# One more up-projection group as seven products, and six operand pairs of the down-projection split by ScalarE and an accumulating DMA inside SBUF

## The chip, the cores and the metric

The kernel runs on one core of one Trainium2 chip. The metric is device time in microseconds (us), the median over several executions; a profile of one further execution goes with it. The engines are named as the profile names them: PE is TensorE (matmuls; PEld is the load of its stationary operand), DVE is VectorE, ACT is ScalarE, POOL is GpSimd, SP is SyncE, which only starts DMAs here.

## The reference

The reference is an encoder trunk of two layers over 512 tokens with a model width of 1024. Each layer has a block of four parallel branches (a convolution and three attentions), which the change does not touch, and then this feed-forward part:

```python
D_MODEL = 1024
SEQ = 512
DEPTH = 2
D_FF = 2816
...
ConvFFN: RMSNorm -> up-projection -> depthwise conv width 3 -> SwiGLU -> down-projection, residual add
```

The up-projection maps the 1024 normalised channels to 2 x 2816, a gate half and an up half. Each of these channels goes through a convolution of width 3 along the tokens. The gate half goes through Silu and is multiplied with the up half, which gives 2816 channels f; the down-projection maps f back to 1024, and the residual is added. All is float32.

## The kernel before

**How a matmul is written.** Operands are split into a high part (a copy that rounds to the fast matmul format) and a low part (the value minus the high part), and each product is made of three matmuls: high by high, high by low, low by high (`prod`, L290 to L292). For every weight unit ACT writes the high part (`w_hi`, L269 or L1277) and DVE the low part (`w_lo`, L271 or L1278), from a staging tile that a DMA has filled. There are three buffers of each, and a unit is asked for two units ahead of its use (`unit`, L275). So PE waits for DVE when a low part comes late.

**The up-projection.** The 2 x 2816 output channels are 22 column tiles of the gate half (s = 0) and 22 of the up half (s = 1). Two neighbouring tiles of both halves are a group; there are 11 groups. A "whole" step (`block`, L308) makes one tile of one half with 24 matmuls of 512 columns; then DVE moves it out of PSUM (L1216, `U<-mm`) and `conv_part` (L1163) runs the convolution: one ACT operation and two of DVE (L1171 to L1173), then Silu on ACT for the gate half (L1177, `fth`), or the product f on DVE for the up half (L1185). A group in `SEVEN` is made by Strassen's scheme instead: seven products of half the size in place of eight, each a step of 24 matmuls of 256 columns (`seven`, L1113, matmul L1130). The sums of its inputs are made once per layer (`seven_forms`, L1071). The sums of its weights are made one after the other in the staging tile, by a DMA from POOL's queue that adds a quarter of the weights to what is there (`grow`, L1258, an accumulating DMA of 512 KB, named `chain<-W` or `w_raw<-W`); high and low parts are split off each time (L1277, L1278). So a group takes 7 x 24 matmuls of 256 columns where the whole form takes 4 x 24 of 512 columns. `UP_STEPS` is the order of all these steps: whole groups 0 and 1, the seven-product groups 2 to 7 interleaved, then the rest whole; the first two blocks after the seven-product groups are made early and held in PSUM.

**The down-projection.** It too runs in Strassen's form, over pairs j = 0 to 10 of two f tiles. The loop over j (`down`, L1369) uses per pair two weight units of 12 matmuls of 512 columns each (L1376 to L1378). Before that, `split_pair` (L1330) makes a pair's operands: three 256-column sums on DVE (L1357 to L1359, and L1363), four copies on ACT for the high parts (L1354) and four subtractions on DVE for the low parts (L1355); two of the four of each are the 512-column halves of the pair itself (`ih`, `kh` high; `il`, `kl` low). For six pairs, those that `EARLY` names by the tile at which they are made, this runs inside the up-projection; for the others it runs in the loop over j, one pair per turn. `pair_tags` (L1313) says in which buffers the operands go: the low parts of a later pair j lie in the buffer `fp{j-1}`, which held the f of pair j - 1.

**What sets the order.** Instructions are put in order per engine by a list scheduler that goes by its own estimates. `first()` (L304) gives those inside it priority. In the second, last layer `turn_res` (L1224) also moves the residual through DVE transposes and 32 DMAs of 64 KB (`resT<-xn`) during the up-projection.

Of the kernel before, what the change touches and what calls it, by code (L numbers as in the profile page):

```python
# [3 lines left out]

# [2 lines left out]

# [5 lines left out]
F32 = mybir.dt.float32  # L15
F32R = mybir.dt.float32r
I32 = mybir.dt.int32
AF = mybir.ActivationFunctionType
ALU = mybir.AluOpType
# [3 lines left out]
P = 128  # L23
L = 2
D = 1024
S = 512
# [3 lines left out]
NF = DFF // P  # L30
# [2 lines left out]

CHUNK = 4

SEVEN = (2, 3, 4, 5, 6, 7)


def up_steps():

    whole = lambda g: [('whole', 2 * g + i, s) for i in range(2) for s in range(2)]
    slots = {}
    for i, g in enumerate(SEVEN):
        for n, at in (('A11', 0), ('S3', 4), ('A22', 6), ('S2', 8), ('A12', 9), ('S1', 10), ('S4', 12)):
            slots[7 * i + at] = ('seven', g, n)
    steps = [w for g in range(SEVEN[0]) for w in whole(g)]
    after = [w for g in range(SEVEN[-1] + 1, NP2) for w in whole(g)]
    own = [slots[t] for t in sorted(slots)]
# [8 lines left out]
              ('gb', 'A22'), ('ga', 'S2'), ('ga', 'S1'), ('gb', 'S2'), ('gb', 'S1'), ('ga', 'S4'), ('gb', 'S4')]  # L57
MIX = (0, 1, 4, 5, 2, 3, 6, 7)

EARLY = (15, 16, 17, 18, 19, 20)  # L60
EPS = 1e-6
BIG = 1e30
EB = 4
# [35 lines left out]
def weight_units():  # L99
# [19 lines left out]
    for g in range(NP2):  # L119
        if g in SEVEN:  # L120
            units.extend(('quarter', (g, r, c), 1024) for r in range(2) for c in range(2))
# [109 lines left out]
class Trunk:  # L231
# [931 lines left out]
    def conv_part(self, i, s):  # L1163

        nc = self.nc
        v = nc.vector
        c = i + s * NF
        u = self.U[s][:, i % 2]
        y = self.fp.tile([P, S], F32, name=f"cy{s}", tag=f"cy{s}", bufs=2)
        w = lambda t: self.par('ffn_conv_w', c * 3 + t)  # L1170
        nc.scalar.activation(y, u[:, 1:513], AF.Identity, scale=w(1), bias=self.par('ffn_conv_b', c))  # L1171
        v.scalar_tensor_tensor(y, u[:, 0:512], w(0), y, ALU.mult, ALU.add)
        v.scalar_tensor_tensor(y, u[:, 2:514], w(2), y, ALU.mult, ALU.add)  # L1173

        if s == 0:
            si = self.fp.tile([P, S], F32, name="fth", tag="fth", bufs=2)
            nc.scalar.activation(si, y, AF.Silu)  # L1177
            self.silus[i] = si
            return
        if self.last and i % 2 == 1 and i // 2 < KT:  # L1180
            self.turn_res(i // 2)
        if i % 2 == 0:
            self.fpair = self.fp.tile([P, 1024], F32, name="f", tag=f"fp{i // 2}", bufs=1)
        fl = self.fpair[:, i % 2 * S:(i % 2 + 1) * S]
        v.tensor_tensor(fl, y, self.silus.pop(i), ALU.mult)  # L1185
        self.F.append(fl)
        if i in EARLY:
            self.split_pair(self.F, EARLY.index(i), self.got)

    def ffn(self, l, last):  # L1190
        nc = self.nc
        v = nc.vector
        self.U = []
        for i in range(2):
            u = self.conv_tile(f"U{i}")
            nc.gpsimd.memset(u[:, :, 0:1], 0.0)
            nc.gpsimd.memset(u[:, :, 513:514], 0.0)
            self.U.append(u)
        self.F, self.got, self.silus, self.sevens, self.last = [], {}, {}, {}, last
        self.seven_forms()  # L1200
        held = {}
        self.pace = 0.0
        for kind, a, b in UP_STEPS:
            if kind == 'seven':
                self.seven(a, b)
                continue
            if kind == 'free':
                ps = held.pop((a, b))
            else:
                ps = self.mm()  # L1210
                self.block(ps)
                self.tick()
            if kind == 'held':
                held[a, b] = ps
            else:
                v.tensor_tensor(self.U[b][:, a % 2, 1:513], ps, self.RB, ALU.mult)  # L1216
                self.conv_part(a, b)
        for g in self.slow:
            for _ in g:
                pass  # L1220
        self.slow = []
        return self.F
# [90 lines left out]
    def pair_tags(self, j):  # L1313

        x = [f"x{n}{d}" for d in range(KT) for n in 'hl']
        late = [(f"lt{n // 2}", n % 2) for n in range(10)]
        hi = [f"fh{2 * j}", f"fh{2 * j + 1}"] if j < len(EARLY) else x[2 * (j - len(EARLY)):][:2]
        lo = ["lo", "lo"] if j == 0 else [(f"fp{j - 1}", 0), (f"fp{j - 1}", 1)]  # L1320
        a = (["e0", "e1"], ["e2", "e3"], ["e4", "e5"], late[0:2], late[2:4], late[4:6],
             ["xr", "xr"], ["xn", "xn"], ["cy0", "cy0"], ["cy1", "cy1"], x[10:12])[j]
        s4 = (late[6:8], late[8:10], ["e6", "e7"], x[12:14], x[14:16], ["t3", "t2"])[j // 2]
        return hi + lo + a + s4

    def conv_tile(self, tag):
# [3 lines left out]
    def split_pair(self, F, j, got):  # L1330

        nc = self.nc
        v = nc.vector
        fi, fk = F[2 * j:2 * j + 2]

        def tile(t):
            if isinstance(t, tuple):
                t, n = t
                if n == 0:
                    self.halves[t] = self.fp.tile([P, 1024], F32R, name=f"p{t}", tag=t, bufs=1)  # L1340
                return self.halves[t][:, n * S:(n + 1) * S]
            pool = self.xpool if t[:2] in ("xh", "xl") else self.fp
            return pool.tile([P, S], F32R, name=f"p{t}", tag=t, bufs=2 if t in ("lo", "xr", "xn", "cy0", "cy1") else 1)

        tags = self.pair_tags(j)
        ih, kh, il, kl, ah, al = (tile(t) for t in tags[:6])
        if j % 2 == 0:
            got['b'] = [tile(t) for t in tags[6:]]
        lo, hi = slice(0, 256), slice(256, 512)
        bh, bl = (t[:, (lo, hi)[j % 2]] for t in got['b'])  # L1350
        a = self.fp.tile([P, S], F32, name="sum", tag="xr" if j < len(EARLY) else "fth", bufs=2)

        def split(h, l, x):
            nc.scalar.activation(h, x, AF.Copy)  # L1354
            v.tensor_tensor(l, x, h.bitcast(F32), ALU.subtract)  # L1355

        v.tensor_tensor(a[:, lo], fi[:, hi], fk[:, hi], ALU.subtract)  # L1357
        v.tensor_tensor(fi[:, hi], fi[:, lo], fi[:, hi], ALU.subtract)
        v.tensor_tensor(a[:, hi], a[:, lo], fi[:, lo], ALU.subtract)  # L1359
        split(ih, il, fi)  # L1360
        split(ah, al, a)
        split(kh, kl, fk)
        v.tensor_tensor(fk[:, lo], fk[:, lo], a[:, hi], ALU.add)  # L1363
        split(bh, bl, fk[:, lo])
        cut = lambda h, l, c: [(h[:, c + b * P:c + (b + 1) * P], l[:, c + b * P:c + (b + 1) * P]) for b in range(2)]
        got[j] = {'a11': cut(ih, il, 0), 's1': cut(ih, il, 256), 'a12': cut(kh, kl, 0), 's4': cut(kh, kl, 256),
                  's3': cut(ah, al, 0), 's2': cut(ah, al, 256), 'a22': cut(bh, bl, 0)}

    def down(self, F, last):  # L1369
# [9 lines left out]

        got, todo = self.got, list(range(len(EARLY), NP2))  # L1380
        A, B = ([self.mm() for _ in range(2)] for _ in range(2))
# [315 lines left out]
```

## Time and profile before

| | us |
|---|---|
| median of three runs | 1542.93 (1542.21 to 1543.67) |
| the profiled execution | 1543.59 |
| its span, first to last instruction | 1541.8 |
| outside the span | 1.79 |
| up-projection of layer 0, from 433.42 to 663.98 | 230.56 |
| up-projection of layer 1, from 1200.20 to 1433.09 | 232.89 |

Times inside the program are counted from the first instruction. T0 below is the end of an up-projection's last matmul and the start of the loop over j. In the windows of the profile a column gives an engine's busy time and in brackets its instructions, then TensorE's granted clock, the busy share of the 16 DMA engines, and what they moved.

### The profile page before, as it was taken

How to read it: one execution, taken by the hardware profiler on the slowest of the kernel's cores; microseconds unless marked ns; L12 is line 12 of the kernel's file. 1: busy time of each engine (PE TensorE's matmuls, PEld its weight loads, DVE VectorE, ACT ScalarE, POOL GpSimd, SP SyncE). 2: the span in 40 equal slices, each digit the busy share in tenths (PEclk: the TensorE clock that was granted, in tenths of full speed). 3: DMA queues.
4: the chain of work that ended last, by engine and by line, in shares of the span. 5: the costliest groups of instructions: out<-in, count | busy, mean ns of one | idle time of the engine just before them, and what ended most of it. 6: DMA issues, size and time to landing. Idle time of an engine off the chain costs nothing.

```text
span 1541.8 us, 22905 instructions
## 1 busy us (share of the span) xinstructions
PE 1528.9 (99%) x8274; PEld 1322.0 (86%) x8274; DVE 1308.0 (85%) x2210; ACT 942.8 (61%) x1580; POOL 187.7 (12%) x288
## 2 busy tenths in 40 slices
PE   9999999999999999999999999999999999999999
PEld 8888888889889999888888888888898899988887
DVE  6689988797789999996576899887986899999974
ACT  6677777356456665564548687673564566655643
POOL 0123002321001110000002130023200011100000
PEclk9999999999999999999999999999999999999999
DMA  7789586856656886366568795867566589852674
GB/s 236 227 229 203 164 181 152 181 151 148 208 168 141 178 182 162 96 205 203 180 185 255 203 202 174 171 161 182 146 150 215 171 173 230 182 155 96 191 229 161
DMA packets 117153, 278.58 MB, mean 181 GB/s; under 512 B 27440, under 2 KB 29360, under 8 KB 117040
## 3 DMA queue, kind: packets, MB, share of 16 engines
q1 hardware_dynamic: 87088, 187.98, 38.2%
q0 software_dynamic: 29664, 88.62, 30.5%
q8 instruction: 65, 1.06, 0.3%
q10 hardware_dynamic: 288, 0.52, 0.1%
q14 instruction: 48, 0.39, 0.1%
HBM read 259.25 MB, written 58.72 MB: 206 GB/s over the span
## 4 chain that ended last, share of the span: by engine, by line
PE 85%; DVE 8%; ACT 3%; issue 2%; DMA 2%; POOL 0%; ACTq 0%; DVEq 0%; POOLq 0%
PE mm L291 14%; PE mm L290 14%; PE mm L292 14%; PE aux L1130 11%; PE aux L936 3%; PE aux L1376 3%; PE aux L1378 3%; PE aux L1377 3%; PE mm L520 2%; PE mm L521 2%; PE mm L522 2%; PE mm L1376 2%; PE mm L1378 2%; PE mm L1377 2%; PE mm L1130 2%
## 5 line engine op out<-in xcount | busy, mean ns | idle before, releaser
L269 ACT ACTIVATE w_hi<-w_raw 128x1024 fp32r<-128x1024 f32 (+1 forms) x241 | 251.1, 1043 | 232.5 <-PE mm L291 83.3
L271 DVE TENSOR_TENSOR w_lo<-w_raw,w_hi 128x1024 fp32r<-128x1024 f32 (+1 forms) x241 | 290.5, 1207 | 72.8 <-ACT w_hi L269 71.3
L290 PE MATMUL mm<-xh,w_hi 128*128 128x512 f32 x768 | 300.2, 391 | 0.0
L291 PE MATMUL mm<-xl,w_hi 128*128 128x512 f32 x768 | 299.5, 390 | 0.0
L292 PE MATMUL mm<-xh,w_lo 128*128 128x512 f32 x768 | 299.3, 390 | 0.0
L292 PEld LDWEIGHTS mm<-xh,w_lo 128*128 128x128 f32 x768 | 144.2, 188 | 30.6
L290 PEld LDWEIGHTS mm<-xh,w_hi 128*128 128x128 f32 x768 | 144.3, 188 | 29.0
L291 PEld LDWEIGHTS mm<-xl,w_hi 128*128 128x128 f32 x768 | 144.3, 188 | 28.3
L1130 PE MATMUL aux<-form,w_hi 128*128 128x256 f32 x768 | 140.2, 283 | 1.4 <-ACT sv L1142 1.4
L1130 PEld LDWEIGHTS aux<-form,w_hi 128*128 128x128 f32 x768 | 120.0, 192 | 2.5 <-ACT sv L1142 2.2
L1130 PE MATMUL aux<-form,w_lo 128*128 128x256 f32 x384 | 108.7, 283 | 0.0
L1277 ACT ACTIVATE w_hi<-chain 128x1024 fp32r<-128x1024 f32 x64 | 67.6, 1057 | 53.7 <-DMA chain<-W 11.5
L457 DVE SCALAR_TENSOR_TENSOR cv<-cv,prm 128x512 f32<-128x512 f32 x120 | 94.6, 788 | 0.7
L1278 DVE TENSOR_TENSOR w_lo<-chain,w_hi 128x1024 fp32r<-128x1024 f32 x64 | 77.9, 1219 | 17.0 <-ACT w_hi L1277 16.7
L1171 ACT ACTIVATE cy<-U,prm 128x512 f32<-128x512 f32 x88 | 68.4, 808 | 32.2 <-DVE U L1216 21.0
L520 PE MATMUL mm<-w_hi,xh 128*128 128x512 f32 x192 | 76.4, 398 | 0.3 <-DVE V L648 0.3
L1277 ACT ACTIVATE w_hi<-w_raw 128x1024 fp32r<-128x1024 f32 x48 | 50.6, 1053 | 42.4 <-PE aux L1130 21.1
L521 PE MATMUL mm<-w_lo,xh 128*128 128x512 f32 x192 | 74.9, 390 | 0.0
L522 PE MATMUL mm<-w_hi,xl 128*128 128x512 f32 x192 | 74.8, 390 | 0.0
L1259 POOL DMA_DIRECT2D chain<-W x48 | 42.1, 876 | 260.4 <-DVE w_lo L1278 233.1
L1130 PEld LDWEIGHTS aux<-form,w_lo 128*128 128x128 f32 x384 | 73.7, 192 | 0.0
L777 ACT ACTIVATE e<-e,rl 128x256 f32<-128x256 f32 (+2 forms) x96 | 57.3, 597 | 21.8 <-DVE rl L776 21.5
(376 smaller groups left out, 3837.7 us busy)
## 6 DMA issues: line engine op xcount, KB each, us to landing
w_raw<-W SPq DMA_DIRECT2D x191, 512.0 KB, 4.1
sums<-W POOLq DMA_DIRECT2D x24, 1024.0 KB, 11.5
chain<-W POOLq DMA_DIRECT2D x48, 512.0 KB, 5.7
w_raw<-W SPq DMA_DIRECT2D x66, 256.0 KB, 3.7
w_raw<-sums SPq DMA_DIRECT2D x44, 256.0 KB, 3.8
w_raw<-sums SPq DMA_DIRECT2D x22, 512.0 KB, 4.3
sums<-W POOLq DMA_DIRECT2D x12, 768.0 KB, 10.7
sums<-sums POOLq DMA_DIRECT2D x8, 1024.0 KB, 7.2
```

The source lines that it names most:

```text
L269: w = nc.scalar.activation(hi[:, s], raw[:, s], AF.Copy)
L271: nc.vector.tensor_tensor(lo[:, s], raw[:, s], hi[:, s].bitcast(F32), ALU.subtract)
L290: mm(ps, lhsT=wh, rhs=xh, start=start, stop=False)
L291: mm(ps, lhsT=wh, rhs=xl, start=False, stop=False)
L292: self.last_mm = mm(ps, lhsT=wl, rhs=xh, start=False, stop=stop)
L457: self.after_mm(v.scalar_tensor_tensor(acc, u[:, t:t + S], w(t), acc, ALU.mult, ALU.add))
L520: mm(pss[b], lhsT=self.Xh[k][:, t], rhs=hi[:, s], start=k == 0, stop=False)
L521: mm(pss[b], lhsT=self.Xh[k][:, t], rhs=lo[:, s], start=False, stop=False)
L522: self.last_mm = mm(pss[b], lhsT=self.Xl[k][:, t], rhs=hi[:, s], start=False, stop=k == KT - 1)
L1130: self.last_mm = nc.tensor.matmul(o, lhsT=w[:, s], rhs=x, start=start and not (e or j or i), stop=j == 3 and i == 2, skip_group_check=True)
L1277: nc.scalar.activation(hi, raw, AF.Copy)
L1278: nc.vector.tensor_tensor(lo, raw, hi.bitcast(F32), ALU.subtract)
```

## The change

1. `SEVEN` takes in group 8 (tiles 16 and 17): in each layer four whole steps go and seven seven-product steps come.
2. `EARLY` becomes a list of steps (tile, half), and the six pairs that are made during the up-projection go through the new `early_pair`. Sums and the operands `ah`, `al`, `bh`, `bl` are made as before. The pair itself is one tile of 1024 columns now: ACT copies it to `hi` and then writes minus `hi` to `low`, and an accumulating DMA of POOL's queue, 512 KB from SBUF to SBUF, adds the pair to `low`. This stands in place of two 512-column copies on ACT and two 512-column subtractions on DVE. The low part of pair j lies in `fp{j-2}` (for pairs 0 and 1 in buffers of their own), and the two halves of the 256-column operand of pair 10 lie in `fp4`.
3. The move out of PSUM of the last four blocks (tiles 20 and 21) stands under `first()`.

```diff
-SEVEN = (2, 3, 4, 5, 6, 7)
+SEVEN = (2, 3, 4, 5, 6, 7, 8)
...
-EARLY = (15, 16, 17, 18, 19, 20)
+EARLY = ((17, 1), (19, 0), (19, 1), (20, 0), (20, 1), (21, 0))
...
-        if i in EARLY:
-            self.split_pair(self.F, EARLY.index(i), self.got)
+        if (i, 1) in EARLY:
+            self.early_pair(EARLY.index((i, 1)))
+
+    def early_pair(self, j):
...
+        f = self.fpairs[j]
+        tags = self.pair_tags(j)
+        hi = self.fp.tile([P, 1024], F32R, name="pfh", tag=f"fh{j}", bufs=1)
+        low = self.fp.tile([P, 1024], F32R, name="plo", tag=f"fp{j - 2}" if j > 1 else f"lo{j}", bufs=1)
...
+        v.tensor_tensor(a[:, :256], q(1), q(3), ALU.subtract)
+        v.tensor_tensor(q(1), q(0), q(1), ALU.subtract)
+        nc.scalar.activation(hi, f, AF.Copy)
+        nc.scalar.activation(low, hi.bitcast(F32), AF.Copy, scale=-1.0)
+        nc.gpsimd.dma_start(low, f, accum_op=ALU.add)
+        v.tensor_tensor(a[:, 256:], a[:, :256], q(0), ALU.subtract)
+        b = self.fp.tile([P, S], F32, name="sum", tag="xr", bufs=2)[:, :256]
+        v.tensor_tensor(b, q(2), a[:, 256:], ALU.add)
+        nc.scalar.activation(ah, a, AF.Copy)
+        v.tensor_tensor(al, a, ah.bitcast(F32), ALU.subtract)
+        nc.scalar.activation(bh, b, AF.Copy)
+        v.tensor_tensor(bl, b, bh.bitcast(F32), ALU.subtract)
...
-                v.tensor_tensor(self.U[b][:, a % 2, 1:513], ps, self.RB, ALU.mult)
+                with self.first() if a >= NF - 2 else nullcontext():
+                    v.tensor_tensor(self.U[b][:, a % 2, 1:513], ps, self.RB, ALU.mult)
...
-        lo = ["lo", "lo"] if j == 0 else [(f"fp{j - 1}", 0), (f"fp{j - 1}", 1)]
+        lo = [(f"fp{j - 1}", 0), (f"fp{j - 1}", 1)]
...
-        s4 = (late[6:8], late[8:10], ["e6", "e7"], x[12:14], x[14:16], ["t3", "t2"])[j // 2]
+        s4 = (late[6:8], late[8:10], ["e6", "e7"], x[12:14], x[14:16], [("fp4", 0), ("fp4", 1)])[j // 2]
```

In the changed kernel the lines of `early_pair` are L1207, L1208, L1212 and L1214 (sums on DVE), L1209 (`pfh`, the high part on ACT), L1210 (`plo`, minus the high part), L1211 (the DMA), L1215 to L1218 (`ah`, `al`, `bh`, `bl`); L1260 moves blocks out of PSUM, L1303 is the weights' accumulating DMA, L1321 and L1322 split the weights of the seven-product steps, and L1390 to L1399 are `split_pair`.

The first place is DVE in layer 0, from the move of the last block out of PSUM to pair 6's low parts, the first that `split_pair` makes in the loop over j. `f_6155` is the f of pair 5 and lies in buffer `fp5`, `f_6400` that of pair 6, and `pfp5` is pair 6's low part, which takes `fp5` over. Before:

```order
L1216 TENSOR_TENSOR U1_4729<-mm_7111,RB_4788 128x512
L1172 SCALAR_TENSOR_TENSOR cy0_7105<-U0_4726,prm_73,cy0_7105 128x512
L1355 TENSOR_TENSOR pfp5_7170<-f_6400,pxl0_7169 128x512
L271 TENSOR_TENSOR w_lo_7208<-w_raw_7206,w_hi_7207 128x1024
L1173 SCALAR_TENSOR_TENSOR cy0_7105<-U0_4726,prm_73,cy0_7105 128x512
L1172 SCALAR_TENSOR_TENSOR cy1_7144<-U1_4729,prm_73,cy1_7144 128x512
L271 TENSOR_TENSOR w_lo_7245<-w_raw_7243,w_hi_7244 128x1024
```

And now, from the 15th row behind that move on; pair 5's last low parts (`plt2`, `pe7`) and four `w_lo` rows stand between the two:

```order
L1216 TENSOR_TENSOR plt2_7184<-sum_7185,plt2_7184 128x512
L271 TENSOR_TENSOR w_lo_7389<-w_raw_7387,w_hi_7388 128x1024
L1218 TENSOR_TENSOR pe7_7130<-sum_7192,pe6_7129 128x256
L1172 SCALAR_TENSOR_TENSOR cy1_7231<-U1_4729,prm_73,cy1_7231 128x512
L1391 TENSOR_TENSOR pfp5_7257<-f_6400,pxh0_7255 128x512
L271 TENSOR_TENSOR w_lo_7407<-w_raw_7405,w_hi_7406 128x1024
L1173 SCALAR_TENSOR_TENSOR cy1_7231<-U1_4729,prm_73,cy1_7231 128x512
```

The pair that is finished last in the up-projection has moved to behind its end, and the first write into `fp5` stands ahead of the low part of loop unit 6 (`w_lo_7407`; units are counted from 0). That write has to wait until pair 5's DMA has read `fp5`.

The second place is ACT in layer 0, at the same stretch, in the changed kernel alone: what it does up to pair 5's `plo`, behind which the DMA is issued.

```order
L1217 ACTIVATE pe6_7129<-sum_7138 128x256
L1177 ACTIVATE fth_7180<-cy0_7176 128x512
L1209 ACTIVATE pfh_7182<-f_6155 128x1024
L269 ACTIVATE w_hi_7349<-w_raw_7348 128x1024
L1210 ACTIVATE plo_7183<-pfh_7182 128x1024
L1215 ACTIVATE plt2_7184<-sum_7185 128x512
L269 ACTIVATE w_hi_7388<-w_raw_7387 128x1024
```

A weight's high part stands between pair 5's high part and minus that part; all of it stands behind the Silu of tile 21.

The third place is ACT in layer 1, in the seven-product groups, where `sv` is the move of a product's PSUM bank that PE needs again. Before:

```order
L1277 ACTIVATE w_hi<-chain 128x1024
L1142 ACTIVATE sv<-aux 128x512
L1277 ACTIVATE w_hi<-chain 128x1024
L1354 ACTIVATE pfh_14987<-f 128x512
L1277 ACTIVATE w_hi<-w_raw 128x1024
L1277 ACTIVATE w_hi<-chain 128x1024
L1142 ACTIVATE sv<-aux 128x512
```

And now:

```order
L1321 ACTIVATE w_hi<-chain 128x1024
L1142 ACTIVATE sv<-aux 128x512
L1321 ACTIVATE w_hi<-chain 128x1024
L1321 ACTIVATE w_hi<-w_raw 128x1024
L1142 ACTIVATE sv<-aux 128x512
L1321 ACTIVATE w_hi<-chain 128x1024
```

The second `sv` has moved ahead of the `w_hi` that stood before it, and the copy of a pair (`pfh`) has gone from between.

More of the change, by code (lines that the diff above doesn't have):

```diff
@@ L7 @@
-from contextlib import ExitStack
+from contextlib import ExitStack, nullcontext
 from itertools import chain
@@ L1178, in conv_part @@
             self.silus[i] = si
+            if (i, 0) in EARLY:
+                self.early_pair(EARLY.index((i, 0)))
             return
@@ L1183, in conv_part @@
             self.fpair = self.fp.tile([P, 1024], F32, name="f", tag=f"fp{i // 2}", bufs=1)
+            self.fpairs.append(self.fpair)
         fl = self.fpair[:, i % 2 * S:(i % 2 + 1) * S]
@@ L1186, in conv_part, with pair_tile @@
         self.F.append(fl)
-        if i in EARLY:
-            self.split_pair(self.F, EARLY.index(i), self.got)
+        if (i, 1) in EARLY:
+            self.early_pair(EARLY.index((i, 1)))
+    def early_pair(self, j):
+        nc = self.nc
+        v = nc.vector
+        f = self.fpairs[j]
+        tags = self.pair_tags(j)
+        hi = self.fp.tile([P, 1024], F32R, name="pfh", tag=f"fh{j}", bufs=1)
+        low = self.fp.tile([P, 1024], F32R, name="plo", tag=f"fp{j - 2}" if j > 1 else f"lo{j}", bufs=1)
+        ah, al = (self.pair_tile(t) for t in tags[4:6])
+        if j % 2 == 0:
+            self.got['b'] = [self.pair_tile(t) for t in tags[6:]]
+        bh, bl = (t[:, j % 2 * 256:j % 2 * 256 + 256] for t in self.got['b'])
+        a = self.fp.tile([P, S], F32, name="sum", tag="xr", bufs=2)
+        q = lambda n: f[:, n * 256:(n + 1) * 256]
+        v.tensor_tensor(a[:, :256], q(1), q(3), ALU.subtract)
[10 more added lines that the diff above has]
+        v.tensor_tensor(bl, b, bh.bitcast(F32), ALU.subtract)
+        cut = lambda h, l, c: [(h[:, c + b * P:c + (b + 1) * P], l[:, c + b * P:c + (b + 1) * P]) for b in range(2)]
+        self.got[j] = {'a11': cut(hi, low, 0), 's1': cut(hi, low, 256), 'a12': cut(hi, low, 512),
+                       's4': cut(hi, low, 768), 's3': cut(ah, al, 0), 's2': cut(ah, al, 256), 'a22': cut(bh, bl, 0)}
+    def pair_tile(self, t):
+        if isinstance(t, tuple):
+            t, n = t
+            if n == 0:
+                self.halves[t] = self.fp.tile([P, 1024], F32R, name=f"p{t}", tag=t, bufs=1)
+            return self.halves[t][:, n * S:(n + 1) * S]
+        pool = self.xpool if t[:2] in ("xh", "xl") else self.fp
+        return pool.tile([P, S], F32R, name=f"p{t}", tag=t, bufs=2 if t in ("xr", "xn", "cy0", "cy1") else 1)
     def ffn(self, l, last):
@@ L1199, in ffn @@
         self.F, self.got, self.silus, self.sevens, self.last = [], {}, {}, {}, last
+        self.fpairs = []
         self.seven_forms()
@@ L1334, in split_pair @@
         fi, fk = F[2 * j:2 * j + 2]
[L1336 to L1343, printed above, removed]
+        tile = self.pair_tile
         tags = self.pair_tags(j)
```

## The prediction

> **What bounds the kernel now.** I began with the page's busy times. PE is busy 99% of the span:
>
> ```profile
> span 1541.8 us, 22905 instructions
> ...
> PE 1528.9 (99%) x8274; PEld 1322.0 (86%) x8274; DVE 1308.0 (85%) x2210; ACT 942.8 (61%) x1580; POOL 187.7 (12%) x288
> ```
>
> So time comes from fewer or shorter PE steps, or from PE's few stalls, and what spares DVE or ACT work counts only where PE waits for it. The change lies in the two feed-forward parts, so next I read windows over their stages, layer 0 first: seven-product steps, the steps up to the last held block, whole steps, down-projection; then the same of layer 1.
>
> ```profile
> core 0: us, PE busy (x) PEld busy (x) DVE busy (x) ACT busy (x) POOL busy (x), PEclk, DMA share, GB/s
> ...
> 480.30:587.10 106.80, 106.79 (x889) 106.59 (x888) 100.72 (x131) 72.64 (x94) 17.53 (x21) 1.00 0.83 180
> 587.10:609.60 22.50, 22.50 (x147) 20.59 (x146) 18.96 (x26) 9.57 (x12) 0.82 (x1) 1.00 0.56 153
> 609.60:664.00 54.40, 54.40 (x242) 45.02 (x242) 54.15 (x89) 31.30 (x45) 0.00 (x0) 1.00 0.34 106
> 664.00:760.00 96.00, 96.00 (x429) 79.49 (x428) 70.83 (x108) 50.35 (x62) 0.00 (x0) 1.00 0.66 210
> ...
> 1247.10:1355.70 108.60, 107.39 (x889) 106.73 (x888) 102.16 (x135) 69.15 (x90) 17.48 (x20) 1.00 0.96 206
> 1355.70:1378.70 23.00, 22.73 (x147) 20.61 (x146) 20.71 (x29) 11.54 (x15) 0.87 (x1) 1.00 0.56 156
> 1378.70:1433.10 54.40, 54.40 (x243) 45.03 (x242) 54.40 (x89) 31.13 (x45) 0.00 (x0) 1.00 0.33 105
> ```
>
> PE has no gap in layer 0, though DVE is full during the whole steps (54.15 of 54.40 us). In layer 1 the same 889 matmuls take 108.60 us against 106.80, and the next 147 take 23.00 against 22.50: PE loses 1.8 + 0.5 = 2.3 us to stalls. The granted clock is 1.00 throughout. For the stalls I read the waits of PE in layer 1's up-projection, and ACT's timeline at the longest:
>
> ```profile
> PE aux L1130 <- ACT sv L1142: 1.4, 2, 1.1
> ```
> ```profile
> 1326.21 1.04 ACT L1277 ACTIVATE w_hi<-w_raw 128x1024 fp32r<-128x1024 f32 x1
> 1330.97 1.06 ACT L1277 ACTIVATE w_hi<-chain 128x1024 fp32r<-128x1024 f32 x1 [3.72 <-DMA chain<-W]
> 1331.94 0.58 ACT L1142 ACTIVATE sv<-aux 128x512 f32<-128x512 f32 x1
> ```
>
> ACT stands 3.72 us at a weight's high part, which waits for an accumulating DMA; the `sv` that PE waits for is queued behind it. The cause lies in the DMA share, 0.96 in this stage and 0.83 in layer 0's.
>
> **The change part by part.** *Group 8 in seven products.* The price of a whole step's matmul, from the groups by line of 609.6 to 664:
>
> ```profile
> L290 PE MATMUL mm<-xh,w_hi 128*128 128x512 f32 x80 | 31.1, 389 | 0.0
> ```
>
> With L291 and L292 alike these are 240 matmuls in 54.40 us, one per 226.7 ns (389 ns is a matmul's own length; they overlap). Four whole steps are 96 x 226.7 = 21.76 us. The seven-product stage has 889 matmuls in 106.80 us, one per 120.1 ns, not half of 226.7, because there the weight loads fill the time (PEld 106.59 of 106.80). Seven steps of 24 are 168 x 120.1 = 20.18 us. So PE has 1.58 us less per layer, 3.2 us in two, all on the path.
>
> *What group 8 adds beside PE*, per layer: seven weight units where there were four, each with one high and one low part, and three `sv`; also four accumulating weight DMAs. The prices, from the groups of 433.4 to 760 on DVE and on ACT:
>
> ```profile
> L1278 DVE TENSOR_TENSOR w_lo<-chain,w_hi 128x1024 fp32r<-128x1024 f32 x24 | 29.3, 1220 | 5.2 <-ACT w_hi L1277 5.0
> ...
> L1355 DVE TENSOR_TENSOR pfp<-f,pfh 128x512 fp32r<-128x512 f32 x10 | 6.7, 682 | 0.0
> ```
> ```profile
> L1277 ACT ACTIVATE w_hi<-chain 128x1024 fp32r<-128x1024 f32 x24 | 25.4, 1060 | 18.6 <-PE aux L1130 6.1 <-issue 4.0 <-PE mm L1130 3.5
> ...
> L1142 ACT ACTIVATE sv<-aux 128x512 f32<-128x512 f32 x18 | 10.5, 582 | 0.0
> L1354 ACT ACTIVATE pfh<-f 128x512 fp32r<-128x512 f32 x12 | 7.5, 624 | 1.3 <-DVE f L1185 1.1 <-DVE f L1358 0.2
> ```
>
> DVE gets 3 x 1.22 and about three more 512-column operations of 0.68, some 5.7 us; ACT gets 3 x 1.06 + 3 x 0.58 = 4.9 us. *The six pairs* take 12 x 0.68 = 8.2 us off DVE, and give ACT 6 x (2 x 1.05 - 2 x 0.62) = 5.2 us. So DVE is 2.5 us the better per layer and ACT, at 31 of 54 us in the whole steps, has room. On the path both are worth nothing: PE had no wait for DVE in these windows, and DVE's relief is cover, not time.
>
> *The moved instructions in layer 1.* The `sv` now stands ahead of the high part that waited. That takes away the longest stall (1.1 us by the waits), if what is late next, the low part of that very weight, is in time: DVE takes 1.2 us for it behind the high part, and the trace shows no wait of PE for it once `sv` had ended. I count 0.9 us gained of the 2.3; the other stalls stay, since the DMAs that cause them do. Below nothing: pair 0's DMA is new in this crowded stretch, behind a weight's DMA in POOL's queue. The stretch against its like in layer 0:
>
> ```profile
> 1250.00:1330.00 80.00, 79.87 (x662) 79.42 (x662) 74.04 (x97) 48.97 (x63) 12.84 (x15) 1.00 1.01 220
> 490.00:570.00 80.00, 80.00 (x669) 80.00 (x668) 75.10 (x96) 52.73 (x68) 13.99 (x16) 1.00 0.84 181
> ```
>
> At a share of 1.01 another 512 KB pushes all behind it; the bounds of this term are -2.3 and +1.5 us.
>
> *Pair 5's DMA, both layers.* This is where the change adds a wait. DVE's first write of pair 6's low part into `fp5` waits for the DMA that reads pair 5 there, and the low part of loop unit 6 is queued behind it; PE reaches this unit at T0 + 6 x 12 x 226.7 ns = T0 + 16.3 us. When does the DMA land? DVE's steps from start to start, from layer 1's timeline, and the start of the last block's move out of PSUM now:
>
> ```profile
> 1330.49 0.42 DVE L1358 TENSOR_TENSOR f<-f 128x256 f32<-128x256 f32 x1
> 1330.83 0.42 DVE L1359 TENSOR_TENSOR sum<-sum,f 128x256 f32<-128x256 f32 x1
> ...
> 1332.06 1.23 DVE L1278 TENSOR_TENSOR w_lo<-chain,w_hi 128x1024 fp32r<-128x1024 f32 x1 [0.48 <-ACT w_hi L1277]
> 1333.25 0.75 DVE L1172 SCALAR_TENSOR_TENSOR cy<-U,prm,cy 128x512 f32<-128x512 f32 x1
> 1333.92 0.68 DVE L1159 TENSOR_TENSOR U<-aux,RB 128x512 f32<-128x512 f32 x1
> 1334.52 0.74 DVE L1173 SCALAR_TENSOR_TENSOR cy<-U,prm,cy 128x512 f32<-128x512 f32 x1
> ```
> ```profile
> 664.21 0.68 DVE L1216 TENSOR_TENSOR U<-mm,RB 128x512 f32<-128x512 f32 x1
> ```
>
> A 256-column operation takes 0.34 us of DVE's time, a low part of a weight 1.19, a convolution step 0.67, a 512-column operation 0.60. That move starts between T0 + 0.2 (as now) and T0 + 0.7 (a row more ahead of it); I take 0.7. From it to pair 5's last sum that ACT needs stand the move, three 256-column operations, one weight, one convolution step and one 512-column operation: 4.1 us, so T0 + 4.8. ACT then has three operations of 1.05 (the pair's copy, a weight, minus the copy): T0 + 8.0. What an accumulating DMA takes, from the line of the weights' in layer 0, then in layer 1, and last of the only transfers inside SBUF, 128 KB each:
>
> ```profile
> L1259 POOL DMA_DIRECT2D chain<-W x18: 863/872/895, 458.6 to 587.0; - x18
> ...
> DMA to landing us min/median/max: 5.3/5.5/6.6
> ```
> ```profile
> DMA to landing us min/median/max: 5.3/5.9/9.2
> ```
> ```profile
> L618 SPq DMA_DIRECT2D KH<-KH x20: 461/474/639, 46.3 to 954.3; - x20
> ...
> DMA to landing us min/median/max: 2.3/5.3/11.3
> ```
>
> I take 5.7 us, from the same size and queue at a DMA share like that behind T0 (0.66 or less): it lands at T0 + 13.7. DVE reaches the waiting row after four weights, three 512-column operations, two convolution steps and ten of 256 columns, 11.3 us: T0 + 12.0. It waits 1.7 us, ends that row at 14.3, and the weight's low part (1.22) at 15.5, 0.8 us before PE needs it. So the DMA has 6.5 us; each microsecond beyond costs PE one, in both layers. I count 0.3 per layer for the error of this sum, 0.6 in all.
>
> The Trainium skill ("DMA: Bandwidth & Descriptors", section on the SWDGE path) fits such a DMA as 2.0 us plus bytes / 436e3, an estimate of 3.2 us for 512 KB. The weights' DMAs of this size took 5.3 at best, so the trace disagrees; by that figure DVE would not wait, and the sum would be 0.6 us lower.
>
> The other five DMAs are not near: pair j's low part is read at T0 + 5.44 j, and the buffer that minus the high part goes into was read by a DMA two steps (10.9 us) before. The move under `first()` takes PSUM free no later than now and costs nothing.
>
> *Sum.* -3.2 - 0.9 + 0.6 = -3.5 us: 1540.1 against the profiled execution's 1543.59 (span 1541.8 and 1.8 around it). That one lies 0.66 above the median of the runs, so against the median it is 1539.4, and I give 1539.5.
>
> **The rivals.** *All stalls go.* With `sv` ahead and no pair copies between, layer 1 runs like layer 0, and pair 5's DMA lands in time: -3.2 - 2.3 = -5.5, 1537.5. Against it: the transfers of the residual still crowd the DMA engines.
>
> *Layer 1 eats part of the gain.* Pair 0's DMA in the crowded stretch delays weights, the stalls stay or grow by up to 1.5 us: -3.2 + 0 to + 1.5, with the 0.6, 1540.3 to 1541.8. For it: the weights' DMA took up to 9.2 us there.
>
> *The DMA inside SBUF is slow* (the other side). It reads SBUF, reads its target and writes it. If it takes L us, the loss is 2 x (L - 6.5). At the longest weights' DMA, 9.2, it is 5.4, and the time 1542.93 - 4.1 + 5.4 = 1544.2; at the longest inside SBUF, 11.3, 9.6 and 1548.4. It decides the sign at L = 8.6, and slower by 0.2% at 10.1. For it: inside SBUF a quarter of the bytes took as long (5.3); against it: those are other, smaller rows among a crowded start.
> The Trainium skill ("SBUF — State Buffer", section "SBUF: two separate sides") has a rule that would bring this about: descriptors of a POOL DMA are not written while DVE holds a port that the two share. The trace shows POOL's issue at 0.87 us with DVE 94% busy, so here it bears little out; no run shows such a DMA beside a DVE that is full.
>
> *The change does not make DVE's relief count*: it is in the forecast already, at nothing.
>
> **How the numbers follow.** Forecast (1538.6 to 1540.3): 0.45. All stalls go: 0.20. Layer 1 eats part: 0.22. Slow DMA (1542.5 to 1548.4): 0.13. About 0.2%, 3.1 us, is what a measurement of this kernel can tell from no change: under 1539.8 is faster, over 1546.0 slower. The forecast lies at the edge and gives 0.27 to faster and 0.18 to same; the first rival gives 0.20 to faster, the second 0.21 to same, and 0.01 to faster, the third 0.07 to same and 0.06 to slower, as 9.2 us is likelier than 11. Together 0.48, 0.46, 0.06. The range goes from the first rival, with 0.3 us for its error, to the slow DMA at 9.0 us: 1537.2 to 1543.8.
>
> **What would show it.** Right: a seven-product stage of layer 0 that is 168 matmuls longer at 120 ns each and whole steps 96 matmuls shorter; `plo<-f` landing in 5 to 6.5 us; DVE idle 1 to 2.5 us before pair 6's first low part with "DMA plo<-f" as releaser; PE without a gap behind T0. Wrong: a landing over 6.5 us with PE waiting for `w_lo` near T0 + 16, PE waits for weights' low parts at either layer's seven-product steps, or a time outside the range.

## The result, and the profile after

The changed kernel takes 1554.67 us (median of six runs, 1549.97 to 1555.57) against 1543.30 for the kernel before (1542.21 to 1544.19): a ratio of 1.0066, 95% interval 1.0049 to 1.0082. It is slower, by some 10 us, where 3.5 us less were forecast. The profiled execution is one of the shorter ones, 1549.97 us with a span of 1548.2 us, 6.4 over the span before.

Where this went is read from the starts of the first and last matmul of each stage, in both traces (us; "down" is the loop over j with the closing units behind it, "between" the rest of both layers):

| stage | before | after | difference |
|---|---|---|---|
| up-projection, layer 0 (from the first seven-product matmul) | 197.47 | 195.87 | -1.60 |
| down-projection, layer 0 | 106.35 | 111.27 | +4.92 |
| up-projection, layer 1 | 199.80 | 196.97 | -2.83 |
| down-projection, layer 1 | 104.49 | 109.79 | +5.30 |
| start, between, tail | 933.71 | 934.27 | +0.56 |

The up-projections gain about what was forecast, 4.43 us in all, and the down-projections lose over twice as much, 10.22 us. The windows of the profile after put the loss into the first 27 us behind T0, which is 663.00 in layer 0 and 1434.01 in layer 1:

```profile
480.30:607.00 126.70, 126.69 (x1053) 126.37 (x1052) 117.46 (x150) 81.80 (x102) 21.93 (x25) 1.00 0.83 183
662.40:680.00 17.60, 17.31 (x77) 14.00 (x75) 12.41 (x22) 14.97 (x21) 1.74 (x2) 1.00 0.97 232
680.00:690.00 10.00, 7.13 (x25) 5.79 (x26) 9.01 (x15) 3.43 (x5) 0.00 (x0) 0.83 0.80 274
690.00:700.00 10.00, 10.00 (x46) 8.28 (x45) 10.00 (x18) 6.41 (x10) 0.00 (x0) 1.00 0.66 226
...
1434.00:1452.00 18.00, 16.71 (x74) 13.51 (x72) 11.91 (x21) 14.46 (x20) 1.74 (x2) 1.00 0.95 241
1452.00:1460.00 8.00, 5.70 (x19) 4.62 (x20) 7.58 (x12) 1.99 (x3) 0.00 (x0) 0.79 0.52 171
```

The same place in layer 0 of the kernel before, where T0 is 663.98:

```profile
664.00:682.00 18.00, 18.00 (x81) 14.92 (x80) 17.99 (x30) 12.81 (x17) 0.00 (x0) 1.00 0.69 221
674.00:684.00 10.00, 10.00 (x46) 8.29 (x45) 10.00 (x18) 6.84 (x10) 0.00 (x0) 1.00 0.90 292
```

In the first row of the profile after, the seven-product steps run as before, 1053 matmuls in 126.70 us. From T0 on the DMA engines are full (0.97 and 0.95), DVE is busy only 12.4 of 17.6 us where it had been full, and then PE is idle and its granted clock falls to 0.83 and 0.79 in the mean of the window. The wait of DVE in that stretch of layer 0, then those of PE over the whole kernel:

```profile
DVE pfp L1391 <- DMA plo<-f: 5.9, 1, 5.9
```
```profile
PE mm L1413 <- DVE w_lo L271: 6.8, 2, 3.6
```

The timelines of ACT, POOL, DVE and PE at this place, one fence each, give the chain:

```profile
670.27 1.05 ACT L1210 ACTIVATE plo<-pfh 128x1024 fp32r<-128x1024 f32 x1
```
```profile
671.61 0.87 POOL L1211 DMA_DIRECT2D plo<-f  x1 [3.75 <-ACT plo L1210]
```
```profile
680.99 0.69 DVE L1391 TENSOR_TENSOR pfp<-f,pxh 128x512 fp32r<-128x512 f32 x1 [5.94 <-DMA plo<-f]
681.60 1.22 DVE L271 TENSOR_TENSOR w_lo<-w_raw,w_hi 128x1024 fp32r<-128x1024 f32 x1
```
```profile
679.32 0.39 PE L1412 MATMUL mm<-w_hi,pfh 128*128 128x512 f32 x1
682.87 0.79 PE L1413 MATMUL mm<-w_lo,pfh 128*128 128x512 f32 x1 [3.16 <-DVE w_lo L271]
683.46 0.63 PE L1414 MATMUL mm<-w_hi,plo 128*128 128x512 f32 x1
683.89 0.63 PE L1412 MATMUL mm<-w_hi,pfh 128*128 128x512 f32 x1
```

Minus pair 5's high part is done at T0 + 8.3, the DMA is issued at T0 + 8.6 and lands 9.28 us later. DVE has stood for 5.94 us when it may write into `fp5`; the low part of loop unit 6 ends at T0 + 19.8, and PE, which was there at T0 + 16.5, has stood for 3.3 us. Behind the wait the matmuls start 427 ns apart (683.46 to 683.89) in place of 227, for some 3 us: 1.6 us more. Layer 1 is the same with a landing of 9.6 us, 3.75 us of idle PE and 1.6 us behind it. This is the chain of the third rival, at the place that it names; why the DMA lands late is another question, which the runs below take up.

### The profile page after: what moved, and what is told of

The parts are those of the page before. It is cut to its first block, busy times and chain, and to the rows that moved or that the text cites. A ratio compares the mean times of both kernels' runs of the same rounds, so it can differ in the third digit from the quotient of the medians.

```text
span 1548.2 us, 23238 instructions
## 1 busy us (share of the span) xinstructions
PE 1529.9 (99%) x8418; PEld 1329.1 (86%) x8418; DVE 1304.4 (84%) x2198; ACT 959.0 (62%) x1592; POOL 204.5 (13%) x308
## 4 chain that ended last, share of the span: by engine, by line
PE 81%; DVE 11%; DMA 3%; issue 2%; ACT 2%; SPq 0%; DVEq 0%; ACTq 0%; POOLq 0%
PE mm L291 12%; PE mm L290 12%; PE mm L292 12%; PE aux L1130 10%; PE aux L936 3%; DVE w_lo L1322 3%; PE mm L520 2%; PE mm L521 2%; PE mm L522 2%; PE aux L1414 2%; PE aux L1412 2%; PE aux L1413 2%; PE aux L813 2%; PE aux L790 2%; DMA plo<-f 2%
## 5 line engine op out<-in xcount | busy, mean ns | idle before, releaser
L290 PE MATMUL mm<-xh,w_hi 128*128 128x512 f32 x704 | 275.3, 391 | 0.0
L291 PE MATMUL mm<-xl,w_hi 128*128 128x512 f32 x704 | 274.6, 390 | 0.0
L292 PE MATMUL mm<-xh,w_lo 128*128 128x512 f32 x704 | 274.4, 390 | 0.0
L1130 PE MATMUL aux<-form,w_hi 128*128 128x256 f32 x896 | 163.5, 283 | 0.1
L292 PEld LDWEIGHTS mm<-xh,w_lo 128*128 128x128 f32 x704 | 132.1, 188 | 28.1
L290 PEld LDWEIGHTS mm<-xh,w_hi 128*128 128x128 f32 x704 | 132.2, 188 | 26.5
L1130 PEld LDWEIGHTS aux<-form,w_hi 128*128 128x128 f32 x896 | 140.0, 192 | 1.0 <-ACT sv L1142 0.7
L1130 PE MATMUL aux<-form,w_lo 128*128 128x256 f32 x448 | 126.9, 283 | 0.0
L1321 ACT ACTIVATE w_hi<-chain 128x1024 fp32r<-128x1024 f32 x72 | 76.1, 1058 | 59.3 <-PE aux L1130 15.5
L1322 DVE TENSOR_TENSOR w_lo<-chain,w_hi 128x1024 fp32r<-128x1024 f32 x72 | 87.7, 1220 | 19.8 <-ACT w_hi L1321 19.4
L1321 ACT ACTIVATE w_hi<-w_raw 128x1024 fp32r<-128x1024 f32 x54 | 57.0, 1055 | 52.8 <-PE aux L1130 29.2
L1130 PEld LDWEIGHTS aux<-form,w_lo 128*128 128x128 f32 x448 | 86.0, 192 | 0.2 <-DVE w_lo L1322 0.2
L1303 POOL DMA_DIRECT2D chain<-W x54 | 47.4, 878 | 280.7 <-DVE w_lo L1322 253.7
L1171 ACT ACTIVATE cy<-U,prm 128x512 f32<-128x512 f32 x88 | 67.7, 806 | 16.3 <-DVE U L1155 9.2
L1322 DVE TENSOR_TENSOR w_lo<-w_raw,w_hi 128x1024 fp32r<-128x1024 f32 x54 | 65.9, 1221 | 6.7 <-ACT w_hi L1321 6.4
```

Of the source, the lines that this page charges most:

```text
L290: mm(ps, lhsT=wh, rhs=xh, start=start, stop=False)
L291: mm(ps, lhsT=wh, rhs=xl, start=False, stop=False)
L292: self.last_mm = mm(ps, lhsT=wl, rhs=xh, start=False, stop=stop)
L1130: self.last_mm = nc.tensor.matmul(o, lhsT=w[:, s], rhs=x, start=start and not (e or j or i), stop=j == 3 and i == 2, skip_group_check=True)
L1321: nc.scalar.activation(hi, raw, AF.Copy)
L1322: nc.vector.tensor_tensor(lo, raw, hi.bitcast(F32), ALU.subtract)
```

## The experiments

Theory A says what the trace says: DVE stands on pair 5's DMA, a weight's low part is queued behind it, PE stalls and then runs slowly. Theory B, its rival, says that the wait is a symptom and the loss comes from group 8's work or the clock. All ratios are against the kernel before, run beside them.

**Pair 5's low part by DVE.** This takes the DMA and its wait away. ACT's writing of minus the high part goes with them, and DVE gets one subtraction of 1.22 us.

```diff
-        nc.scalar.activation(low, hi.bitcast(F32), AF.Copy, scale=-1.0)
-        nc.gpsimd.dma_start(low, f, accum_op=ALU.add)
+        if j == 5:
+            v.tensor_tensor(low, f, hi.bitcast(F32), ALU.subtract)
+        else:
+            nc.scalar.activation(low, hi.bitcast(F32), AF.Copy, scale=-1.0)
+            nc.gpsimd.dma_start(low, f, accum_op=ALU.add)
```

> Pair 5's low part is made by a DVE subtraction of 1024 columns; pairs 0 to 4 keep the DMA. Theory A: no PE wait behind T0 in either layer, no clock loss, so the 3.3 and 3.75 us stalls and about 1.8 us of slow clock behind each go: 1539 to 1540.5, faster than before by 0.15 to 0.3%. Theory B: within 2 us of the changed kernel.

1540.65 us, ratio 0.9982 (0.9973 to 0.9990). The down-projections take 106.41 and 104.49 us, as before the change, and the up-projections 195.87 and 196.93, as after it. The same stretches in its windows:

```profile
662.80:680.00 17.20, 17.20 (x77) 14.27 (x76) 17.13 (x28) 14.12 (x21) 0.87 (x1) 1.00 0.94 261
680.00:690.00 10.00, 10.00 (x45) 8.26 (x44) 10.00 (x17) 6.62 (x10) 0.00 (x0) 1.00 0.89 326
```

DVE and PE are full and the clock is 1.00, though the DMA engines are as busy as in the changed kernel. So one DMA of the six in each layer costs all of the loss, and what is left, 2.8 us by the ratio, is near the forecast's gain of 3.5. Theory A holds for the changed kernel.

**Pair 6's low part into another buffer.** DVE then waits for pair 4's DMA, issued 4.6 us sooner.

```diff
-        lo = [(f"fp{j - 1}", 0), (f"fp{j - 1}", 1)]
+        lo = [(f"fp{4 if j == 6 else j - 1}", n) for n in range(2)]
...
-             ... [("fp4", 0), ("fp4", 1)])[j // 2]
+             ... [("fp5", 0), ("fp5", 1)])[j // 2]
```

> Pair 6's low part goes into fp4 in place of fp5, and pair 10's operand into fp5, so DVE waits for pair 4's DMA and not for pair 5's. Theory A (DVE stands on a pair's DMA, a weight's low part behind it comes late, PE stalls and then runs at half clock for some us): in layer 0 pair 4's DMA lands at about T0 + 10, before DVE is there, so that layer's stall goes (-5 us against the change); in layer 1 pair 4's DMA landed at T0 + 15, so a stall of 2 to 3 us stays there: 1544 to 1546. Theory B (the loss comes from group 8 or from a lower clock under more work, and the wait is only a symptom): as the changed kernel, 1550 to 1555.

1548.24 us, ratio 1.0029 (1.0019 to 1.0038). Layer 0 is free of the loss (106.41 us; DVE waits 1.1). In layer 1 pair 4's DMA landed after 10.94 us, DVE waited 5.3, PE 3.74, and the down-projection took 111.60 us. The mechanism came out as expected in each layer; the time was 2.2 us over the range that I wrote, as PE's wait in layer 1 was longer and was followed by 12 matmuls 427 ns apart.

**Group 8 alone**, with the pairs split by DVE as before (the edit is the line of `SEVEN`).

> The kernel before with only group 8 added to the seven-product groups; the pairs are split by DVE as before. Theory A: the PE arithmetic alone, -3.2 us, with layer 1's stalls somewhere between as before and gone: 1538.5 to 1540.5, if the fuller DVE is in time. Theory B: no gain or a loss, 1543 and over.

1547.62 us, ratio 1.0024 (1.0016 to 1.0033), slower. Theory A's number is missed by 7 us, and theory B's (1543 and over) came true: group 8's work alone does cost time. It is another loss than the changed kernel's, which goes with one DMA. The up-projection of layer 0 gains only 0.21 us (197.26). Its waits of PE from 600 to 760, and in layer 1 from 1380 on:

```profile
PE mm L290 <- DVE U L1216: 1.1, 1, 1.1
```
```profile
PE mm L290 <- DVE U L1216: 1.8, 1, 1.8
PE aux L1377 <- DVE w_lo L271: 0.2, 1, 0.2
```

A whole step waits for a PSUM bank that DVE has not emptied yet. DVE is full there (31.97 of 32.00 us from 632 on), and the three more low parts of weights per layer have no room. The step that waits is the first of the last four, so the bank holds an earlier step than those whose move the change puts under priority. So the new splitting of the pairs is not for nothing: it pays for group 8. Between this kernel and the one with pair 5 by DVE lie 7 us.

**The pairs alone**, with group 8 as four whole steps (the line of `SEVEN` put back).

> The new splitting of the six pairs and the early move out of PSUM, with group 8 as four whole steps. Theory A: pair 5's DMA is late as in the change, so before plus 10.5 us of stalls and slow clock: 1552 to 1555, PE waits of 3 to 4 us per layer for w_lo. Theory B: near before, 1542 to 1545.

1545.42 us, ratio 1.0009 (1.0000 to 1.0018): theory A's number is missed by 6.6 us and more, and theory B's range (1542 to 1545) nearly met. The source view of the DMA's line in layer 0, for pair 5:

```profile
L1211 POOL DMA_DIRECT2D plo<-f x1: 869/869/869, 664.0 to 664.0; - x1
...
  DVE pfp L1391: 0.6, 1
...
DMA to landing us min/median/max: 4.6/4.6/4.6
```

T0 is 664.51 in this kernel: the DMA is issued 0.5 us ahead of it, 9 us sooner than in the change, and lands in 4.6 us. In layer 1 it is issued at T0, lands after 7.6, DVE waits 3.3 and PE 1.87. So the late DMA is no property of the new splitting; group 8 as seven products moves the last pair's work behind T0, into the loop's own transfers. The loss behind T0 needs both parts of the change, and in that theory A as I wrote it was too narrow.

**The changed kernel again**, for its times.

> The changed kernel itself once more, beside the next three and for its two groups of times (1550.0 and 1554.3 to 1555.6). Theory A, with the clock: the longer runs have a longer stretch at half clock behind the same stalls, or a stall that another transfer order makes longer; the profile shows granted clock below 1.00 only behind T0. Rival: the granted clock is lower all along in the longer runs.

1552.42 us (1550.55 to 1556.60), ratio 1.0059 (1.0045 to 1.0072); the profiled execution took 1552.61. It has the same two losses (111.55 and 110.41 us) and the same low clock behind them only; 1.7 of its 2.6 us over the first profile lie in layer 1's up-projection, 198.70 against 196.97 us for the same instructions. An execution of 1555 us was not traced. The record gives those of 1554 us and over a mean granted clock of 0.995 or 0.996, and the two of 1550 us 0.998: by these means, an estimate, about twice the time at half clock. Where they lose it stays open.

**The six pairs one step earlier.**

```diff
-EARLY = ((17, 1), (19, 0), (19, 1), (20, 0), (20, 1), (21, 0))
+EARLY = ((17, 0), (17, 1), (19, 0), (19, 1), (20, 0), (20, 1))
```

> The six pairs are made one step earlier, so pair 5's DMA is issued about 5 us sooner, near T0 + 3. Theory A (the wait is late because the DMA is issued late): it lands by T0 + 13 or so and PE stalls not at all or under 1 us per layer, without a clock loss: 1539 to 1542. Rival (the DMA's latency rules, whatever its issue): it lands as late as before, since it meets the same transfers: 1546 and over.

1541.65 us, ratio 0.9989 (0.9981 to 0.9998): the time that was expected, but not for the reason given. The DMA was issued at T0 + 8.0, only 0.6 sooner, and took 8.80 us. In the order of DVE, though, the low part of unit 6 now stands ahead of the write into `fp5`:

```profile
674.98 1.21 DVE L271 TENSOR_TENSOR w_lo<-w_raw,w_hi 128x1024 fp32r<-128x1024 f32 x1
676.12 0.68 DVE L1188 TENSOR_TENSOR f<-cy,fth 128x512 f32<-128x512 f32 x1
676.72 0.41 DVE L1395 TENSOR_TENSOR sum<-sum,f 128x256 f32<-128x256 f32 x1
679.81 0.69 DVE L1391 TENSOR_TENSOR pfp<-f,pxh 128x512 fp32r<-128x512 f32 x1 [2.68 <-DMA plo<-f]
```

DVE waits 2.68 us and PE does not wait at all in layer 0 (106.39 us); in layer 1 it waits 0.5. What was queued behind the wait set the price.

**Pair 5's early work under the priority.**

```diff
-                self.early_pair(EARLY.index((i, 0)))
+                with self.first() if i == 21 else nullcontext():
+                    self.early_pair(EARLY.index((i, 0)))
```

> The whole of pair 5's early work stands under the priority that the move out of PSUM has; all DMAs stay. In the order this brings pair 5's DMA forward by little, but DVE's first write into fp5 now stands behind the low parts of loop units 6 and 7 and not ahead of unit 6's. If what is queued behind the wait decides (theory A'), DVE still waits for the DMA, 1 to 3 us, but PE has no stall over 0.5 us at unit 6 and no slow clock: 1540 to 1542. If the DMA's lateness by itself decides, the loss moves to unit 8 and the time is 1546 or over.

1541.81 us, ratio 0.9985 (0.9975 to 0.9994). All DMAs stay, and pair 5's takes 7.9 and 10.8 us; with the low parts of units 6 and 7 ahead of the waiting row the down-projections take 106.35 and 105.80 us. In layer 0 DVE did not wait for the DMA at all, against what I wrote: it reached that row at T0 + 18.0, after the landing at T0 + 15.5. In layer 1 it waited 0.5 us, and the landing of 10.8 us, longer than any of pair 5's in the change, went with a loss of only 1.3 us. This agrees with the reading of the run before.

**The residual's loads held back.** In layer 0 six loads of 256 KB start just behind T0, in layer 1 four; here they wait for the matmuls of loop turn 4.

```diff
+            if j == 5:
...
+                if last:
+                    for b, h in ((2, 0), (3, 0), (0, 0), (1, 0)):
+                        self.paced(nc.sync.dma_start(us[b // 2][:, b % 2, :S], self.resT[b * P:(b + 1) * P, h * S:(h + 1) * S]))
+                else:
+                    for d in range(6):
+                        xr.append(self.fp.tile([P, S], F32, name="xr", tag=f"e{d}", bufs=1))
+                        self.paced(nc.sync.dma_start(xr[d], self.xres[d]))
```

> The loads of the residual that start just behind T0 (six of 256 KB in layer 0, four in layer 1) wait until loop unit 10, so they don't meet pair 5's DMA. Theory C (these loads make that DMA slow): it lands in about 7 us in place of 9.3 and 9.6, PE stalls 0.5 to 1.5 us per layer, no clock loss: 1541 to 1544. Rival (the pair's own DMA before it and the weights' loads do): it lands as late as now in both layers, and the time is that of the changed kernel.

1547.94 us, ratio 1.0027 (1.0017 to 1.0038). Pair 5's DMA lands in 8.1 and 7.9 us, between the two accounts; PE stalls 2.1 and 2.65 us. So these loads explain 1.2 and 1.8 us of the landing, as far as one trace of each tells (the changed kernel's own two traces differ by 0.4 and 0.2).

**Pair 4's low part by DVE, pair 5's by the DMA** (the edit of the first experiment with j == 4).

> Pair 4's low part by DVE, pair 5's by the DMA, so that no accumulating DMA is in flight within 10 us ahead of pair 5's. If two of them beside the loop's loads made pair 5's slow, it lands in 6 to 7.5 us in layer 0 (9.3 now); if the loads alone do, in 9 us as now. The waiting row stands behind unit 7's low part here, so the time is 1540 to 1542.5 either way, and only the landing tells.

Pair 5's DMA took 8.63 us in both layers, against 9.3 and 9.6, though issued 3 us later in layer 0 and 4 in layer 1, among other loads: as far as the two stretches compare, the DMA ahead of it explains 1 us at most, and the loop's loads the larger part. No run takes the weights' loads of the loop away, so their share stays argued. The time expected was missed: 1546.29 us, ratio 1.0023 (1.0014 to 1.0032). The later issue, T0 + 11.6 in layer 0, brought a DVE wait of 4.1 us behind unit 7, and PE stalled 1.45 us at a later unit in layer 0, 2.07 in layer 1.

**Work for PE in the wait.** Sixteen matmuls with zeros stand ahead of the one that waits.

```diff
+            for _ in range(fill):
+                mm(ps[:, :256], lhsT=x[0], rhs=none, start=False, stop=False, skip_group_check=True)
```

> Sixteen matmuls of 256 columns with an operand of zeros, 1.9 us in all, stand ahead of the matmul that waits in loop unit 6; they add nothing to the sums. If the half clock comes from the length of PE's idle time, the idle falls from 3.3 and 3.75 us to 1.4 and 1.8, no slow matmuls follow, and the kernel is 3 to 4 us faster than the changed one although it does more. If the clock has nothing to do with that stall, the time is as the changed kernel's.

1553.03 us, ratio 1.0058 (1.0045 to 1.0070), as the changed kernel. The first half of the expectation came true: PE idles 1.2 us in place of 3.2, and no slow matmul follows:

```profile
679.89 2.07 PE L1414 MATMUL mm<-none,pfh 128*128 128x256 f32 x16
683.19 0.50 PE L1415 MATMUL mm<-w_lo,pfh 128*128 128x512 f32 x1 [1.22 <-DVE w_lo L271]
683.52 0.39 PE L1416 MATMUL mm<-w_hi,plo 128*128 128x512 f32 x1
```

But the time is not 3 to 4 us less, and the down-projection of layer 0 takes 111.78 us (111.27 in the changed kernel). In both layers PE now waits once more 10 us on, also for a weight's low part (waits from 660 to 760):

```profile
PE aux L1415 <- DVE w_lo L271: 1.6, 1, 1.6
PE mm L1415 <- DVE w_lo L271: 1.2, 1, 1.2
```

DVE had lost its 5.9 us, is full in the units behind (10.00 of 10.00 us in the window from 690 of the changed kernel), and cannot keep up with a PE at full clock. So in layer 0 the slow clock cost nothing that DVE would not have taken. Layer 1 compares less well: its DMA landed sooner here, after 7.7 us.

**Pairs 0 and 5 by DVE** (the first experiment's condition as `j in (0, 5)`), which asks for the rest.

> As the kernel with pair 5's low part by DVE, and pair 0's low part by DVE too; pair 0's DMA stood in layer 1's crowded stretch and landed after 11 to 12.6 us there. If that DMA delays weights there, layer 1's up-projection falls from 196.9 us to 196.0 to 196.5 and the time to 1539.8 to 1540.4; if the residual's transfers alone make the stretch slow, the time stays at 1540.6.

1540.85 us, ratio 0.9979 (0.9970 to 0.9989): no difference from pair 5 alone. Layer 1's up-projection took 197.42 us (196.93 with pair 5 alone), so pair 0's DMA is not what makes that stretch slow. That the residual's transfers do is not shown, as no run takes them away there.

## Why the prediction was wrong

- *PE's arithmetic, -1.58 us per layer*: right; layer 0's up-projection is 1.60 us shorter, wherever DVE is relieved.
- *DVE's relief worth nothing on the path, but cover*: right as far as the change goes, and the price without that cover, which I did not give, is in the run with group 8 alone: 7 us against the kernel with pair 5 by DVE.
- *Layer 1's stalls, -0.9 us*: of that size in the first profile (-2.83 less the arithmetic, -1.2), but not shown: in the ten traces of kernels with group 8 and the new splitting the same stage took 196.93 to 200.77 us, 198.70 in the changed kernel's second, so a gain of 0.9 is lost in the spread.
- *Pair 5's DMA, "I take 5.7 us, from the same size and queue at a DMA share like that behind T0 (0.66 or less)"*: this step failed. All around it was right: the issue (T0 + 8.0 worked out, 8.6 measured), DVE at the waiting row (12.0; 12.05), PE at unit 6 (16.3; 16.5). But 0.66 is the mean over the 96 us of the down-projection, and the 10 us from 674 to 684 of the kernel before, where this DMA lands, had 0.90, with the residual's and the weights' loads in them. With the new DMAs it is 0.97, and the landing 9.3 and 9.6 us. Nor was the row taken at 0.66 or less: 16 of its 18 DMAs were issued in the stage that the prediction itself shows at 0.83, and layer 1's 5.9 us comes from one at 0.96. So the share alone does not give the landing. What was in flight beside it differed: with the weights' DMA issued at 526.7 in the kernel before (5.9 us), SP's queue took 9.5% of the engines' time and moved 0.22 MB; with pair 5's (671.6 to 680.9 in the changed kernel) it took 65.1% and moved 1.83 MB. That these loads make it late is shown in part, by the run that holds the residual's back. The row that was nearest in size and queue came from another stretch.
- *The price beyond 6.5 us, one for one and layer*: too low. By it a landing of 9.3 and 9.6 costs 5.9 us in all; it cost 4.92 + 5.30. PE's stalls, 3.3 and 3.75 us, came out near it; the 1.6 us behind each were not in the sum. Each layer's loss is near DVE's own wait (5.9 and 6.3 us): 1 us less here, and from 1.1 less to 0.4 more in the three other traces with the waiting row in this place (the changed kernel again, the residual's loads held back, work for PE). I had counted the slack of one unit and not that DVE is full for some 20 us behind it, so that its lost time is not made good.
- *The range*: the rival was named with its place and got 13%; its upper end in the text, 1548.4, would also have been short. Its reason, a DMA that is slow inside SBUF, is not what the runs show: alone it landed in 4.6 to 4.8 us. (`KH<-KH` is not the only transfer inside SBUF, as the prediction has it: `KL<-KL` is of the same size, with a median of 6.0 us. The bound of 11.3 stands.)

By the fit in the Trainium skill ("DMA: Bandwidth & Descriptors", section "Anatomy of one DMA") 512 KB take 3.2 us, an estimate; these DMAs took 4.6 us alone and up to 12.6 beside others, so it does not carry over. The Trainium skill's rule of a port that DVE holds ("SBUF — State Buffer", section "SBUF: two separate sides") is not what made them late: pair 2's was issued at 652.88 while DVE was busy 32.52 of 32.60 us, in 0.88 us, and landed after 4.8, while pair 5's stayed in flight from 675.10 to 680.90 with DVE doing nothing (0.00 of 5.80 us).

## What to carry to other kernels

A DMA in place of an engine's work is priced by the transfers that it meets where it runs. So what other queues move is read over the microseconds in which it would be in flight, and not the DMA share of its stage. Then look at what frees its source: the first writer into that buffer waits, and what matters most is what is queued behind that writer on an engine that is full; moving the waiting row behind one urgent row was worth almost all of the loss. A part that loses alone can gain when another part pays for its engine: group 8 alone was 0.24% slower, and with the new splitting (pair 5's by DVE) 0.18% faster.

## What the runs showed of the hardware

An accumulating DMA takes one and a half to two times the engines' time of a plain one. The DMA view of 652 to 658.5 of the changed kernel holds one of them and about as many bytes of plain loads:

```profile
q0 software_dynamic: 144, 0.52, 45.5%
q1 hardware_dynamic: 245, 0.46, 21.3%
...
plo<-f POOLq DMA_DIRECT2D x1, 512.0 KB, 4.8
```

45.5% of 6.5 us is 3.0 us of all 16 engines for 0.52 MB, 21.3% is 1.4 us for 0.46 MB. The plain loads are SP's; a plain copy of POOL's own queue (`xf<-res`, from 421.6 to 425.4 in the kernel before) took 26.0% of 3.8 us, 1.0 us for 0.26 MB. Inside SBUF, alone, an accumulating DMA lands sooner (4.6 to 4.8 us) than from outside (5.1 at best).

PE's clock halves after a short idle. In four executions PE stood for 2.1 to 4.1 us at one matmul (seven cases), and 5 to 12 matmuls at or soon behind it came 427 ns apart; behind waits of 1.2 to 2.07 us (eleven cases in the feed-forward parts) none did. The price comes in fixed pieces: the granted clock is 0.50 for 3.41 us at each stall of the changed kernel (from 682.51 and from 1453.92) and for 6.83 us in the run with pair 6's low part in another buffer. The fall need not come while PE stands: with the residual's loads held back, PE went on at 681.80 in layer 0 and the clock fell at 682.77. The Trainium skill ("TensorE: Matmul & The Clock Gate", section "Part 1: The HAM clock gate") names an idle window of about 3.4 us; here 2.1 us were enough.
